# A hybrid encoder trunk on one core: gated attention as two streams, local attention divided by its sums at the gates

## The chip, the cores and the metric

The kernel runs on one core of a Trainium2 chip. The metric is the device time of one execution in microseconds; the kernel before takes 2370.76 us, the median of 3 runs (2369.61 to 2370.84). The core has five engines with a queue each: TensorE (PE in the profile, with PEld for its weight loads), VectorE (DVE), ScalarE (ACT), GpSimd (POOL) and SyncE (SP). SP issues all DMAs of this kernel, in the order of the program.

## The reference, cut to what matters

Two layers act on two sequences, 2048 and 512 tokens of width 1024. The even layer has one input projection, two parallel attention branches and one output projection; the odd layer is a gated short convolution.

```python
# branch A: gated linear attention, 4 heads of 128, in both directions
b = jnp.cumsum(gi, axis=2)                      # log decay within a chunk
inter = einsum('bhcd,bhde->bhce', qi * exp(b), S)
intra = einsum('bhij,bhje->bhie', scores, vi)   # scores: q_i . (k_j * exp(b_i - b_j))
S_new = exp(b_last) * S + einsum(..., ki * exp(b_last - b), vi)
# branch B: local attention over |i-j| <= 128, 8 heads of 64, 2 key heads
e = jnp.exp(s - m)
p = e / (jnp.sum(e, -1, keepdims=True) + jnp.exp(sk - m))
o = jnp.einsum('bnkgqs,bnskd->bnqkgd', p, vb)
return o * jax.nn.silu(z)                       # the gate
# then
x = layer_norm(DN_ALPHA * x + concatenate([ya, yb]) @ w_out)
```

The dividing by the sum in branch B can be done before the product with the values, as here, or behind it, since each query has one sum for each head.

## The kernel before, in words

All 2560 tokens are laid end to end: groups 0 to 3 (512 tokens each) are the long sequence and group 4 is the short one; a chunk `c` is 128 tokens, 20 in all.

**Dense stages.** `run` lists them in order: for groups 4, 3, 2, 1 a token stage (`tok`, values and decay inputs, weights 336 wide) and a channel stage (`ch`, 21 weight units), then the output projection of group 4 (`oe`), `tok` and `ch` of group 0, the odd layer of group 4 (`one`), `oe` 0, `oo` 4, `oe` 1, `oe` 2, then pairs of groups through the odd layer (`pair`) with the remaining `oe` and `oo`. Each dense product is made of three matmuls in fp32r, high by high, high by low and low by high. A weight unit is loaded by SP (`ws`), its high half cast by ScalarE (`wh`, three buffers) and its low half subtracted by GpSimd (`wl`, two buffers); `dense_ch` and `dense_tok` use them. What a dense stage puts out goes through PSUM banks (`acc`, four, and `ps`, four) and through the eight middle buffers `md` to DRAM.

**The order of the work** is written by a planner in Python while the program is built. `Model` keeps a clock for each engine from rough costs. The dense generator is the main stream; at each of its `yield`s `Flow.pump` lets side generators go on, those whose tiles are ready by the model and whose rank comes first (rank 0: preparing inputs; 1: gated attention; 2: local attention and the rest). `flow.defer` puts a step off until its tiles are written by the model. So PE's order is fixed in the program, and the hardware follows it with semaphores.

**Gated attention** (`gla_stream`, `inside`, lines 1186 to 1382, 1454 to 1491). Chunks go backwards, 19 to 16 and then 15 to 0. `inside` does a whole chunk: seven levels (block sizes 1 to 64), in which VectorE multiplies the decays into the queries `QQ` and the keys `KK` and PE forms scores block by block in small matmuls, 32 columns wide; then the keys are turned (`turn`), multiplied with the values (`grow`) and the state of the backward direction is brought on. `QQ`, `KK` have one buffer each, so a chunk's levels begin when the chunk before is through. Then `along` goes forward through the chunks and writes the mixed, gated output.

**Local attention** (`swa_front`, `swa_back`, lines 1510 to 1664). For each of 20 chunks and 2 key heads, `swa_front` makes the scores of four heads in `Pt`, their maximum, the exponentials and sums `den`, takes the reciprocal, and VectorE multiplies the probabilities by it, head by head. `swa_back` turns the probabilities on PE, splits them, multiplies them with the values, and GpSimd multiplies the two heads' outputs `o` by the gate `gb`. At most two blocks wait between them (`self.blocks`).

**Buffers** touched: `e2p` (one each of `QQ`, `KK`, `tA`, `v` and others, two `km`, four `P`), the four wide buffers `y` of `yp` (also: residual rows, some weights of the token stages, the decay projection's weights `up` and inputs `G`), and the eight `md`.

Of the kernel before, what the change touches and what calls it, by code (L numbers as in the profile page):

```python
# [22 lines left out]
NC = T // 128  # L23
# [239 lines left out]
class Flow:  # L263
# [113 lines left out]
class Trunk:  # L377
    def __init__(self, tc, nc, I, y_out, ctx):
# [23 lines left out]
        self.vb_s = dr("vb_s", (NC, 128, 256))  # L402
        self.qf_s = dr("qf_s", (NC, 128, 512))
# [10 lines left out]
        self.blocks = []  # L414
# [154 lines left out]
    def dense_ch(self, xh, xl, w=None, last=True):  # L569

        nc = self.nc
        wh, wl = w or self.weight()
        p = self.pd()
        for k in range(8):
            c = slice(k * 128, k * 128 + 128)
            nc.tensor.matmul(p[:], wh[:, c], xh(k), start=(k == 0), stop=False)
            nc.tensor.matmul(p[:], wh[:, c], xl(k), start=False, stop=False)
            yield
        if last:
            self.drop(wh)  # L580
            self.cook()
        for k in range(8):
            c = slice(k * 128, k * 128 + 128)
            nc.tensor.matmul(p[:], wl[:, c], xh(k), start=False, stop=(k == 7))
            if k % 2 and k < 7:
                yield
        if last:
            self.drop(wl)
        return p
# [86 lines left out]
    def setup(self):  # L676
        nc, c = self.nc, self.const
        nc.scalar.preload_act_table_set("natural_log_exp_and_others")
        load = self.load
        self.ident = load("ident", (128, 128))  # L680
        self.hl = load("hl", (128, 2))
        self.norm_g = load("norm_g", (128, 1))
        self.eps = c.tile([128, 2], F32, name="eps")
        nc.vector.memset(self.eps[:, 0:1], LN_EPS)
        nc.vector.memset(self.eps[:, 1:2], NORM_EPS)
        self.dtot = c.tile([128, NC, 4], F32, name="dtot")
        self.one = c.tile([128, 1], F32, name="one")
        nc.vector.memset(self.one[:], 1.0)
# [490 lines left out]

    def gla_load_k(self, c):  # L1180
        K = self.e((128, 2, 512), "KK")
# [4 lines left out]
    def inside(self, c, first, last, ld, K, ahead):  # L1186
# [3 lines left out]
        Q = self.e((128, 2, 512), "QQ")  # L1190
# [10 lines left out]

        acmp = self.sm((128, 4, 32), "acmp")
# [17 lines left out]
        def grow_k(s):  # L1220
# [12 lines left out]
        Sb = self.bst if not last else None  # L1233
        wait = []
        for li, s in enumerate((1, 2, 4, 8, 16, 32, 64)):
            n = 512 // s
            pls = []
            if s in (8,):
                qm = self.m2(hold=True)
                nc.scalar.copy(qm[:].rearrange("p (b two s) -> p b two s", two=2, s=s), halves(Q, s))  # L1240
                wait.append((li, s, qm))
            else:
# [14 lines left out]
                for lt, t, qm in wait:  # L1257
# [3 lines left out]
                    self.drop(qm)  # L1261
# [24 lines left out]
                kms.pop(s, None)  # L1286
# [36 lines left out]
        nc.vector.tensor_copy(self.dtot[:, c], mk(end, 4, [[1, 4]]))  # L1323
        ahead(0)
        self.flow.defer(lambda: nc.sync.dma_start(self.qf_s[c], Q[:, 1]), Q)

        def turn(i):
# [3 lines left out]
            t = self.e((128, 4, 128), "km", bufs=2)  # L1331
# [3 lines left out]
        def grow(t):  # L1335
            pv = self.pw((128, 4, 128))
            for h in range(4):
                nc.tensor.matmul(pv[:, h], t[:, h], v[:, h * 128:h * 128 + 128], start=True, stop=True)
            return pv

        kf = kb = None
        if not last:
            yield from self.bank()
# [5 lines left out]
                                  acmp[:].unsqueeze(2).broadcast_to(wide))  # L1349
        if not first:  # L1350
            yield from self.bank()
            kb = turn(1)
        ahead(1)
# [10 lines left out]
        if not first:  # L1364
# [6 lines left out]
            else:  # L1371
                for h in range(4):
                    nc.vector.scalar_tensor_tensor(Sn[:, h], Sb[:, h], mk(end, h, [[1, 1]]), pv[:, h],
# [8 lines left out]
        yield [Q]  # L1382
# [19 lines left out]
    def along(self, c, first, last, ld, ahead):  # L1402
# [13 lines left out]
        if not last:  # L1416
# [4 lines left out]
            else:  # L1421
                for h in range(4):
                    nc.vector.scalar_tensor_tensor(Sn[:, h], Sf[:, h], self.dtot[:, c, h:h + 1], m[:, h],
# [29 lines left out]

    def gla_stream(self):
        for g in (4, 3, 2, 1, 0):
# [3 lines left out]
            cs = list(range(4 * g + 3, 4 * g - 1, -1))  # L1459
            ld, K = self.gla_load(cs[0]), self.gla_load_k(cs[0])  # L1460
            nxt = {}
            for i, c in enumerate(cs):
                yield [*ld, K]

                def ahead(n):
                    if i < 3:
                        nxt[n] = (self.gla_load, self.gla_load_k)[n](cs[i + 1])
                yield from self.inside(c, *ends(c), ld, K, ahead)
                ld, K = nxt.get(0), nxt.get(1)
            if 4 * g > c0:  # L1470
                continue
            self.bst = None
            ld = K = None
            nxt.clear()
# [35 lines left out]
    def swa_front(self):  # L1510
# [16 lines left out]
        while left:  # L1527
# [10 lines left out]
            for kv in range(2):  # L1538
# [3 lines left out]
                Pt = self.e((128, 4, 385), "P", bufs=4)  # L1542
# [36 lines left out]
    def swa_back(self):  # L1579
# [17 lines left out]
        for n in range(40):  # L1597
# [4 lines left out]
            if kv == 0:  # L1602
# [3 lines left out]
                gb, o = load(c)  # L1606
            yield [Pt]
# [26 lines left out]
            yield [pl, V]  # L1634
            Pt = None
# [15 lines left out]
            yield [gb]  # L1651
# [451 lines left out]
    def run(self):  # L2103
# [70 lines left out]
        flow.add(self.swa_front())  # L2174
        flow.add(self.swa_back())
# [29 lines left out]
```

## Time and profile before

| what | value |
|---|---|
| median of 3 runs | 2370.76 us |
| the profiled execution, its own time | 2370.12 us |
| its span, first to last instruction | 2368.1 us |
| mean granted clock of TensorE | 0.998 |
| instructions | 43087 |

The page of the profile lists busy times by engine and by groups of instructions; other views answer by stretch of time, by tile, by wait. Nearly all instructions carry line 242 (the helper that notes every operation for the planner), so groups are told apart by the tiles' names: `wl<-ws,wh` is the subtraction for a weight's low half, `acc<-st,wh` a dense matmul, `ps<-QQ,km` a matmul of a level, `P<-P,den` the scaling of probabilities.

### The profile page before, as it was taken

The page shows a single profiled execution, that of the slowest core. Times are in us where ns is not written, and L with a number is a line of the kernel's source. Part 1 is how long each engine was busy: PE and PEld are TensorE (multiplying, and loading weights), DVE is VectorE, ACT ScalarE, POOL GpSimd, SP SyncE. Part 2 cuts the span into 40 slices and gives each one's busy share as a digit, 9 for nine tenths or more (in the row PEclk, how much of TensorE's full clock was granted, in tenths as well). Part 3 has the DMA queues.
Part 4 walks back from the last instruction along what each step waited for, and adds up shares of the span by engine and source line. Part 5 has one row for each costly group of instructions (what it writes and reads, how often), then busy time and mean ns, then how long its engine had stood idle before and what let it go on. Part 6 is the DMA issues. An engine that isn't in the chain of part 4 may idle for free.

```text
span 2368.1 us, 43087 instructions
## 1 busy us (share of the span) xinstructions
PE 2343.9 (99%) x15830; PEld 1951.8 (82%) x15830; DVE 1582.8 (67%) x2699; ACT 1226.1 (52%) x2363; POOL 1418.4 (60%) x1610
## 2 busy tenths in 40 slices
PE   8999999999999999999999999999999999999998
PEld 8888889888988888888888888878888877888887
DVE  2267756767767677577776467876566587656567
ACT  4666776656576645665577532543334343333431
POOL 5454435443444444444444467898887689988674
PEclk9999999999999999999999999999999999999999
DMA  7977686676667657675478777232124633221573
GB/s 230 295 226 233 221 269 229 209 221 221 218 194 236 223 173 242 197 218 161 158 245 268 266 261 243 92 116 89 52 78 140 217 105 103 73 72 58 175 242 121
DMA packets 275057, 437.37 MB, mean 185 GB/s; under 512 B 21360, under 2 KB 160240, under 8 KB 274848
## 3 DMA queue, kind: packets, MB, share of 16 engines
q1 hardware_dynamic: 274848, 434.64, 56.5%
q8 instruction: 125, 2.05, 0.4%
q14 instruction: 84, 0.69, 0.1%
HBM read 319.72 MB, written 114.84 MB: 184 GB/s over the span
## 4 chain that ended last, share of the span: by engine, by line
PE 87%; DVE 5%; POOL 4%; DMA 2%; issue 1%; ACT 1%; SPq 0%; POOLq 0%; DVEq 0%; ACTq 0%
PE acc L242 71%; PE ps L242 17%; POOL wl L242 1%; POOL wh L242 1%; DVE st L242 1%; DVE bst L242 1%; DVE y L242 1%; POOL md L242 0%; SPq L242 0%; DVE QQ L242 0%; DVE P L242 0%; DVE KK L242 0%; DMA K<-kb_s 0%; DMA mix_s<-gb 0%; DMA op_s<-QQ 0%
## 5 line engine op out<-in xcount | busy, mean ns | idle before, releaser
L242 POOL TENSOR_TENSOR wl<-ws,wh 128x256 fp32r<-128x256 f32 (+1 forms) x912 | 750.7, 855 | 711.4 <-PE acc L242 478.0
L242 PE MATMUL acc<-st,wh 128*128 128x512 f32 x3160 | 828.5, 395 | 2.8 <-DVE pr L242 2.0
L242 PEld LDWEIGHTS acc<-st,wh 128*128 128x128 f32 x3160 | 580.9, 188 | 121.0 <-issue 3.1
L242 PE MATMUL acc<-st,wl 128*128 128x512 f32 x1744 | 471.9, 395 | 2.8 <-POOL wl L242 1.9
L242 PE MATMUL acc<-wh,st 128*128 128x512 f32 (+1 forms) x1680 | 389.4, 371 | 7.9 <-ACT st L242 6.4
L242 PEld LDWEIGHTS acc<-st,wl 128*128 128x128 f32 x1744 | 320.8, 188 | 68.0 <-POOL wl L242 4.1
L242 PEld LDWEIGHTS acc<-wh,st 128*128 128x128 f32 x1680 | 300.2, 189 | 55.1 <-ACT st L242 6.4
L242 ACT CAST wh<-ws 128x1024 fp32r<-128x1024 f32 (+2 forms) x252 | 249.0, 989 | 184.2 <-DMA ws<-in_w_oo 55.9
L242 PE MATMUL acc<-wl,st 128*128 128x512 f32 (+1 forms) x840 | 209.0, 368 | 0.6 <-POOL wl L242 0.5
L242 ACT ACTIVATE md<-md 128x512 f32<-128x512 f32 x264 | 164.7, 631 | 20.5 <-DVE md L242 14.9
L242 PEld LDWEIGHTS acc<-wl,st 128*128 128x128 f32 x840 | 150.7, 188 | 23.8 <-POOL wl L242 1.3
L242 DVE SCALAR_TENSOR_TENSOR md<-acc,md 128x512 f32<-128x512 f32 (+1 forms) x113 | 77.0, 683 | 81.5 <-ACT md L242 76.5
L242 DVE TENSOR_TENSOR st<-pr,st 128x512 fp32r<-128x512 f32 x115 | 98.5, 874 | 41.6 <-ACT st L242 41.2
L242 ACT ACTIVATE md<-acc 128x512 f32<-128x512 f32 (+1 forms) x133 | 76.2, 597 | 67.0 <-PE acc L242 66.5
L242 POOL TENSOR_TENSOR wh<-md,wh 128x256 fp32r<-128x256 f32 x118 | 96.7, 842 | 13.6 <-ACT wh L242 13.1
L242 ACT CAST pth<-ps 128x512 fp32r<-128x512 f32 x112 | 65.3, 583 | 73.1 <-PE ps L242 72.3
L242 DVE CUSTOM_DVE_ANT_0 P<-ps,P 128x384 f32<-128x384 f32 (+1 forms) x160 | 79.3, 525 | 29.6 <-PE ps L242 29.0
L242 ACT ACTIVATE P<-P,nm 128x385 f32<-128x385 f32 (+1 forms) x160 | 93.2, 587 | 3.9 <-DVE nm L242 3.9
L242 ACT ACTIVATE mv<-mv,eps 128x1 f32<-128x1 f32 x40 | 11.8, 295 | 151.8 <-DVE mv L242 147.7
L242 PE MATMUL acc<-P,wh 128*128 128x512 f32 x312 | 89.5, 400 | 0.4 <-POOL wh L242 0.4
L242 ACT COPY km<-KK 128x512 f32<-128x512 f32 x80 | 50.8, 635 | 72.2 <-DVE KK L242 50.9
L242 ACT CAST st<-pr 128x512 fp32r<-128x512 f32 x115 | 68.3, 617 | 30.3 <-DMA pr<-mix_s 12.9
(490 smaller groups left out, 4090.2 us busy)
## 6 DMA issues: line engine op xcount, KB each, us to landing
ws<-in_w_ch SPq DMA_DIRECT2D x105, 512.0 KB, 4.4
ws<-in_w_od SPq DMA_DIRECT2D x58, 512.0 KB, 4.2
ws<-in_w_oe SPq DMA_DIRECT2D x40, 512.0 KB, 3.8
ws<-in_w_oo SPq DMA_DIRECT2D x36, 512.0 KB, 3.5
K<-kb_s SPq DMA_DIRECT2D x32, 384.0 KB, 6.3
d_s<-md SPq DMA_DIRECT2D x40, 256.0 KB, 4.2
qb_s<-md SPq DMA_DIRECT2D x80, 128.0 KB, 3.9
tA<-d_s SPq DMA_DIRECT2D x20, 512.0 KB, 5.7
```

Source lines behind the costliest of these rows:

```text
L242: r = f(*a, **k)
```

## The change

1. **Two streams for gated attention.** `inside` ends after the levels and the copy of the totals; it puts the chunk on `self.heads`. A new stream `gla_behind` takes it from there through `behind` (turned keys, values, states). At most two chunks may be open (`self.open`).
2. **Buffers for that.** Keys and queries are taken and dropped explicitly; `gla_home` gives their own buffer or, where that is taken, one of the wide `y` buffers, though not between the end of group 1's projections and the loading of the residual rows of group 4. Compacted keys `km` may also lie in `md`; the turned keys always do.
3. **Loads.** The next chunk's decays are loaded at level 4 and its keys at level 32, across group borders where the inputs are there; values are loaded by the second stream.
4. **Local attention divides at the gates.** The four multiplies on `Pt` go. The reciprocals go to DRAM (`rd_s`) by one DMA for each block, and `swa_back` loads them broadcast over 64 partitions by four DMAs for each block into a buffer of `md`; GpSimd multiplies the gate by it before the multiply with `o`.
5. **Ranks.** Both streams of gated attention and both of local attention have rank 1.
6. **The planner.** `flush` looks each late step up again before it runs it, and `dense_ch` holds its bank until it is done.

```diff
     def flush(self, everything=False, name=None):
-        now, keep = [], []
-        for one in self.late:
-            (now if everything or name in one[2] or (name is None and one[0] <= self.t) else keep).append(one)
-        self.late = self.model.late = keep
+        now = [one for one in self.late if everything or name in one[2] or (name is None and one[0] <= self.t)]
         for one in now:
-            one[1]()
+            if any(one is x for x in self.late):
+                self.late[:] = [x for x in self.late if x is not one]
+                one[1]()
...
+    def gla_home(self, tag):
+
+        done = self.flow.done
+        rows = "swa_in1" in done and "res_x1_4_3" not in done
+        return [(self.e2, tag, 1)] if rows or self.model.spare(tag, 1) else self.large[:1]
+
     def gla_load_k(self, c):
-        K = self.e((128, 2, 512), "KK")
+        K = self.take(self.gla_home("KK"), (128, 2, 512))
...
-        Q = self.e((128, 2, 512), "QQ")
+        while self.free_at(self.gla_home("QQ")) > self.flow.t:
+            yield 0.3
+        Q = self.take(self.gla_home("QQ"), (128, 2, 512))
...
+        while self.open > 1:
+            yield 0.3
+        self.open += 1
...
-                    km = kms[2 * s] = self.e((128, 512), "km", bufs=2)
+                    km = kms[2 * s] = self.take([(self.e2, "km", 2)] + self.mids, (128, 512))
...
-            if s == 4:
-                v = self.e((128, 512), "v")
-                nc.sync.dma_start(v[:], self.v_s[c])
+            if s in (4, 32):
+                ahead(s)
             yield [Q] if s < 16 else [Q, K]
-        end = tots[128]
+        nc.vector.tensor_copy(self.dtot[:, c], mk(tots[128], 0, [[1, 8]]))
+        self.heads.append((c, first, last, K, Q, base, acmp))
+        self.flow.mark("head_%d" % c)
...
+    def behind(self, c, first, last, K, Q, base, acmp, v, ahead):
...
-            t = self.e((128, 4, 128), "km", bufs=2)
+            t = self.m2((128, 4, 128), hold=True)
             nc.scalar.copy(t[:], pt[:])
...
+    def gla_behind(self):
+        nxt = []
+        for c in [*range(19, 15, -1), *range(15, -1, -1)]:
+            yield "head_%d" % c
+            v = nxt.pop() if nxt else self.load_v(c)
...
+            yield from self.behind(*self.heads.pop(0), v, ahead)
...
-                Pt = self.e((128, 4, 385), "P", bufs=4)
+                Pt = self.new(self.e2, (128, 4, 385), F32, "P", 4, True)
...
                 nc.vector.reciprocal(den[:], den[:])
-                for h in range(4):
-                    nc.vector.tensor_scalar(Pt[:, h, :w], Pt[:, h, :w], den[:, h:h + 1], None, op0=ALU.mult)
-                    if h == 1:
-                        yield []
+                nc.sync.dma_start(self.rd_s[c, kv].rearrange("h t -> t h"), den[:])
...
+            if kv == 0:
+                rb = self.m2(hold=True)
+            for j in range(4):
+                nc.sync.dma_start(rb[64 * kv:64 * kv + 64, 128 * j:128 * j + 128],
+                                  self.rd_s[c, kv, j:j + 1].broadcast_to([64, 128]))
...
-            yield [gb]
+            yield [gb, rb]
+            flat = gb[:].rearrange("p h t -> p (h t)")
+            nc.gpsimd.tensor_tensor(flat, flat, rb[:], op=ALU.mult)
+            self.drop(rb)
+            yield [o]
             nc.gpsimd.tensor_tensor(gb[:], o[:], gb[:], op=ALU.mult)
...
         flow.add(self.gla_stream(), rank=1)
-        flow.add(self.swa_front())
-        flow.add(self.swa_back())
+        flow.add(self.gla_behind(), rank=1)
+        flow.add(self.swa_front(), rank=1)
+        flow.add(self.swa_back(), rank=1)
```

More of the change, by code (lines that the diff above doesn't have):

```diff
@@ L413, in __init__ @@
         self.bst = None
-        self.blocks = []
+        self.blocks, self.heads, self.open = [], [], 0
         self.x, self.owned, self.refs, self.pairs, self.wblocks = {}, {}, {}, {}, {}
@@ L572, in dense_ch @@
         wh, wl = w or self.weight()
-        p = self.pd()
+        p = self.pd(hold=True)
         for k in range(8):
@@ L1232, in inside @@
         base = None
-        Sb = self.bst if not last else None
         wait = []
@@ L1338, in grow, with place @@
                 nc.tensor.matmul(pv[:, h], t[:, h], v[:, h * 128:h * 128 + 128], start=True, stop=True)
+            self.drop(t)
             return pv
+        def place():
+            yield from self.bank()
+            while self.free_at(self.mids) > self.flow.t:
+                yield 0.3
         kf = kb = None
         if not last:
-            yield from self.bank()
+            yield from place()
             kf = turn(0)
@@ L1349, in inside @@
                                   acmp[:].unsqueeze(2).broadcast_to(wide))
+        self.open -= 1
         if not first:
-            yield from self.bank()
+            yield from place()
             kb = turn(1)
-        ahead(1)
+        self.drop(K)
         yield [A, v] + ([Sb] if Sb is not None else [])
@@ L1452, in seq, with ahead @@
         return (0, 16) if g < 4 else (16, 20)
+    def gla_behind(self):
[3 more added lines that the diff above has]
+            v = nxt.pop() if nxt else self.load_v(c)
+            def ahead():
+                if c not in (0, 16) and "gla_in%d" % ((c - 1) // 4) in self.flow.done:
+                    nxt.append(self.load_v(c - 1))
+            yield from self.behind(*self.heads.pop(0), v, ahead)
+            v = None
     def gla_stream(self):
+        nxt = {}
         for g in (4, 3, 2, 1, 0):
```

56 lines of the change are left out of this document (38 added, 18 removed).

## The prediction

> **What bounds the kernel now.** I read the page first: the span, the busy row, the chain that ended last, and the counts of DMA packets.
>
> ```profile
> span 2368.1 us, 43087 instructions
> ...
> PE 2343.9 (99%) x15830; PEld 1951.8 (82%) x15830; DVE 1582.8 (67%) x2699; ACT 1226.1 (52%) x2363; POOL 1418.4 (60%) x1610
> ...
> DMA packets 275057, 437.37 MB, mean 185 GB/s; under 512 B 21360, under 2 KB 160240, under 8 KB 274848
> ...
> q1 hardware_dynamic: 274848, 434.64, 56.5%
> ...
> PE 87%; DVE 5%; POOL 4%; DMA 2%; issue 1%; ACT 1%; SPq 0%; POOLq 0%; DVEq 0%; ACTq 0%
> ```
>
> PE is busy for 2343.9 of 2368.1 us, so all its idle time is 24.2 us, and 87% of the chain is PE. An average over stages hides where the 24.2 us lie, so next comes the view by stretches (columns: window, us, busy us and instruction count of PE, PEld, DVE, ACT, POOL, then clock, DMA share, GB/s). Below it stand the first and the last group of attention's matmuls, by their tiles (ns least/median/most, first and last start): they run from 121.9 to 1357.3 us.
>
> ```profile
> 0.00:100.00 100.00, 93.40 (x460) 81.24 (x461) 25.78 (x47) 55.74 (x89) 54.53 (x84) 1.00 0.81 251
> 100.00:1300.00 1200.00, 1198.14 (x10694) 1008.12 (x10693) 842.75 (x1767) 755.15 (x1577) 536.47 (x672) 1.00 0.69 220
> ...
> 1500.00:1600.00 100.00, 97.00 (x412) 77.67 (x411) 81.40 (x95) 41.97 (x73) 92.28 (x86) 0.98 0.26 90
> ...
> 1900.00:2000.00 100.00, 96.45 (x423) 77.35 (x423) 87.74 (x103) 40.60 (x75) 91.21 (x85) 1.00 0.28 96
> ...
> 2300.00:2368.00 68.00, 60.20 (x263) 48.91 (x261) 43.70 (x61) 12.56 (x27) 31.78 (x37) 0.97 0.40 145
> ...
> L242 PE MATMUL ps<-qn,KK x640: 196/196/218, 121.9 to 1140.9; 128*32 128x32 f32 x160
> L242 PE MATMUL ps<-ident,km x80: 270/272/273, 320.9 to 1357.3; 128*128 128x128 f32 x80
> ```
>
> This is the main reading. In the 1200 us in which attention runs, PE idles 1200 − 1198.14 = 1.86 us. The rest of its idle time is the first load (6.6), the tail (7.8), and two places of 3.0 and 3.55 us in the pair stages. VectorE, with 843 of 1200 us, has room. What PE waited for says the same (us in total, times, longest):
>
> ```profile
> PE acc L242 <- ACT st L242: 6.4, 1, 6.4
> PE acc L242 <- POOL wl L242: 2.4, 3, 1.1
> ```
>
> No row names an attention tile at over 1 us. Attention is filler between the dense matmuls, and filler that finishes sooner shortens nothing unless something dense waits for it. Its first consumer in the last stretch is the output projection of group 0, whose input is loaded from the mixed values (SP row) and used by PE (second row) at:
>
> ```profile
> 1263.46 1.60 SPq L242 DMA_DIRECT2D pr<-mix_s  x3
> ...
> 1319.65 2.54 PE L242 MATMUL acc<-wh,st 128*128 128x512 f32 x10
> ```
>
> The load is issued 56 us before PE turns to that stage, and PE is still in the stage before until then. Attention being earlier is worth nothing there; being later costs something only after some 50 us.
>
> **The change part by part.** *PE.* No matmul, transpose or weight load is removed or added: levels, turned keys, values, states and the eight-head scores keep their counts, so the 15830 stay. That term is 0.
>
> *Order on PE.* Two chunks may now be open and local attention is sorted by ready time beside them. The price of mixing is in the time line: eight dense matmuls take 1.98 us after others like them, and 2.11 us after a burst of small ones.
>
> ```profile
> 539.79 1.98 PE L242 MATMUL acc<-st,wh 128*128 128x512 f32 x8
> ...
> 541.70 0.46 PE L242 MATMUL ps<-qn,KK 128*32 128x32 f32 x32
> 541.97 0.56 PE L242 MATMUL ps<-QQ,KK 128*32 128x32 f32 x32
> 542.46 2.11 PE L242 MATMUL acc<-st,wh 128*128 128x512 f32 x8
> ...
> L242 PE MATMUL ps<-QQ,KK 128*32 128x32 f32 (+1 forms) x1600 | 34.1, 210 | 0.1
> L242 PE MATMUL ps<-QQ,km 128*32 128x32 f32 x1920 | 28.1, 199 | 1.1 <-ACT pth L242 0.7 <-DVE acmp L242 0.2 <-DVE QQ L242 0.2
> L242 PE MATMUL ps<-qn,KK 128*32 128x32 f32 x640 | 9.2, 199 | 0.0
> L242 PE MATMUL ps<-md,km 128*32 128x32 f32 x640 | 9.2, 199 | 0.0
> ```
>
> That is 0.13 us for each return. The four groups have 4800 small matmuls; in bursts of 32 these are at most 150 returns, 20 us. But the levels of one chunk still follow each other in one stream, and the other stream has only wide matmuls, so bursts can hardly meet more often. I take 0, with a quarter of the 20 us as the bound each way (an estimate): −5 to +5.
>
> *VectorE.* The scaling of the probabilities goes, and on the page of the attention stretch with shapes kept apart it is two rows. The sums' reciprocals stay.
>
> ```profile
> L242 DVE TENSOR_SCALAR P<-P,den 128x384 f32<-128x384 f32 x128 | 61.6, 543 | 1.1
> L242 DVE TENSOR_SCALAR P<-P,den 128x256 f32<-128x256 f32 x32 | 10.9, 405 | 0.3
> ...
> L242 POOL TENSOR_TENSOR wl<-ws,wh 128x256 fp32r<-128x256 f32 x564 | 459.8, 847 | 541.3 <-PE acc L242 385.4 <-ACT wh L242 103.9 <-ACT km L242 9.8
> L242 POOL TENSOR_TENSOR gb<-gb 128x512 f32<-128x512 f32 x20 | 27.3, 1367 | 61.4 <-DVE gb L242 61.4
> ```
>
> So 61.6 + 10.9 = 72.5 us leave an engine that PE does not wait for: worth 0 up to the 1.86 us of idle time. I take −0.5. The copy of the totals takes eight columns for four: nothing.
>
> *GpSimd.* A multiply of 128x512 is added for each of 20 chunks: 20 × 1.367 = 27.3 us. Queued behind it are the subtractions that make the weights' low halves, and PE waits for those. But GpSimd stands idle for 385.4 us in front of them until PE gives a buffer back, so 1.4 us at a time lies beside that: 0. Were this cover gone it would be the whole 27.3. The new multiply waits for gates and factors only, and stands ahead of the old one, which waits 61.4 us in 15 places for VectorE; some of it fills that.
>
> *SP's queue.* This is the one new wait with something behind it. For each of 40 blocks one store of the reciprocals is issued at once, not deferred, so SP stands until the reciprocal is done; and four broadcast loads follow (160 in all), which must wait until the store has landed. 200 issues at the 0.33 to 0.62 us of the rows below (a fifth of 3.11) are 66 to 124 us more on SP. Behind them stand the loads of weights: for those ScalarE's cast waits, then GpSimd, then PE. How late may a weight load be? One unit, followed through four engines:
>
> ```profile
> 543.17 0.33 SPq L242 DMA_DIRECT2D ws<-in_w_ch  x1
> ...
> 549.31 1.04 ACT L242 CAST wh<-ws 128x1024 fp32r<-128x1024 f32 x1
> ...
> 554.02 3.89 POOL L242 TENSOR_TENSOR wl<-ws,wh 128x256 fp32r<-128x256 f32 x4 [4.21 <-PE acc L242]
> ...
> 564.86 0.62 PE L242 MATMUL acc<-st,wl 128*128 128x512 f32 x2
> ...
> ws<-in_w_ch SPq DMA_DIRECT2D x105, 512.0 KB, 4.4
> ...
> 709.21 3.11 SPq L242 DMA_DIRECT2D kb_s<-md  x5
> ...
> SPq L242 <- DVE den L242: 9.1, 3, 4.5
> SPq L242 <- POOL wl L242: 490.1, 195, 7.4
> ...
> DMA to landing us min/median/max: 2.7/4.7/6.7
> ```
>
> It lands at 543.2 + 4.4 = 547.6; the cast could wait 1.7 us more for it; between cast and subtraction lie 554.02 − 550.35 = 3.7 us; between subtraction and use 564.86 − 557.91 = 6.9 us. Together 12.3 us of cover. The new wait is bounded by 4.5 us (the longest that SP now waits for a den tile) plus a landing of 4.7, the median of the mixed values' transfers: about 9 us, and nothing where the block lies queued first. Waits of SP up to 7.4 us are there already, 195 of them, and PE does not feel them. So the wide stages hide it. The four token stages after the first have narrower weights and less cover: of 40 blocks over some 1070 us, about 6 fall into their 4 × 40 us. From 0 to 6 × 4 us; I take a quarter of a microsecond each, +1.5.
>
> The Trainium skill speaks against this store: its page "DMA: Bandwidth & Descriptors", section "Specifications", says that transfers under 512 B are read, changed and written back. The store has 512 pieces of 4 B, and the 20480 new ones would nearly double the page's 21360 packets under 512 B. At the price of an average packet here, 0.565 × 16 × 2368.1 us / 274848 = 78 ns, one store takes 512 × 78 / 16 = 2.5 us, and the landing 7.2. The wait is then 11.7 us, just inside the cover, and the sum by this rule would be about 2 us higher. No row here prices such a piece.
>
> *Buffers.* Keys and queries take a second home among the four wide buffers (y), the compacted keys, the turned keys and the factors come from the eight middle ones (md). These also take what the dense stages put out. An eviction that finds none free holds ScalarE and then a bank; today no bank is waited for longer than the rows above. I take 0; the upper bound is the second rival.
>
> *The planner's own edits* (late work run once, the dense bank held, one rank) issue nothing. Their effect is in the order, bounded above.
>
> **Sum.** The profiled execution took 2370.1 us, 2.0 outside its span; the median of the runs is 0.6 above it. 2370.1 + 0 − 0.5 + 0 + 1.5 + 0 = 2371.1. I write **2371 us**: no change that can be told.
>
> **Rivals.** *The pair stages gain* (faster): with attention done sooner, buffers come free and both stalls go, 3.0 + 3.55 us, and with the granted clock of 0.98 in the first of them another 2: 2371 − 8.5 = 2362. Against it: the second stall, at 1900 to 2000, has the same size with no attention for 500 us, and both follow GpSimd's load (92 and 91%).
>
> *SP's queue starves PE* (slower). Place: the store that waits for the reciprocal and the loads that wait for the store. It decides when the two waits of successive blocks fall on one weight, over 12 us. If in half of the 40 blocks PE is left 0.8 us without weights, that is 16 us: 2387. For it: SP is strictly in order, and the planner knows nothing of a wait in DRAM. Against: the cover above.
>
> *The wide buffers* (slower). The residual rows of the first output projection need all four of them:
>
> ```profile
> L242 SPq DMA_DIRECT2D y<-in_x x4: 423/425/498, 763.9 to 800.5; - x4
> ...
> L242 DVE SCALAR_TENSOR_TENSOR y<-y,acc x6: 669/683/690, 825.2 to 869.4; 128x512 f32<-128x512 f32 x6
> ```
>
> The last row is loaded 25 us before its first use. It decides if keys or queries hold such a buffer past 825: the dense stream then stands, some 10 to 20 us, 2381 to 2391. The change bars keys and queries from them before that stage, which speaks against it. A stall of this length would also cost clock: in the stretch 1500 to 1600, with 3.0 us idle, the granted clock fell to 0.98.
>
> *It doesn't speed attention up*: the streams wait for the dense stage that makes their input, or for each other. The time is the same 2371, since nothing dense waits for it.
>
> **How the numbers follow.** A measurement of this kernel tells about 0.2%, 4.7 us, from no change, so "same" is 2366.0 to 2375.5. No change, whether attention is sooner or not: 0.46. The pair stages, or an order that is luckier by about as much: 0.24. SP's queue 0.18, the buffers 0.12. So faster 0.24, same 0.46, slower 0.30. The range goes from 2359 (the faster case with the lower bound of the order) to 2388 (SP's case), which leaves out the far half of each.
>
> **What would show it.** Right: 15830 matmuls; PE idle in the attention stretch under 5 us; VectorE 70 us less busy; GpSimd 27 us more; the last attention matmul before 1357 and the pair stage starting where it does. Wrong: rows in which PE waits for the casts, the subtractions or the wide buffers for over 5 us in sum; SP waiting for a landing of the reciprocals for over 12 us; or fewer or cheaper dense matmuls in the attention stretch, which I exclude.

## The result, and the profile after

The changed kernel takes 2528.82 us (median of six runs, 2521.07 to 2536.77) against 2370.03 us for the kernel before (six runs, 2369.05 to 2370.84). The ratio is 1.0668, with a 95% interval of 1.0644 to 1.0692: 159 us slower. The prediction was 2371 us in a range of 2359 to 2388, so it was wrong, by far more than the range.

The profiled execution took 2522.22 us. Its page, in the same lines as before (the last is the traffic of SP's queue: packets, MB, share of 16 DMA engines):

```profile
span 2520.4 us, 43271 instructions
...
PE 2389.7 (95%) x15830; PEld 1980.6 (79%) x15830; DVE 1507.1 (60%) x2539; ACT 1224.8 (49%) x2364; POOL 1442.3 (57%) x1630
...
DMA packets 309124, 442.74 MB, mean 176 GB/s; under 512 B 45056, under 2 KB 194432, under 8 KB 308912
...
q1 hardware_dynamic: 308912, 439.98, 61.5%
```

PE does the same 15830 matmuls. Its idle time went from 24.2 to 2520.4 − 2389.7 = 130.7 us, 106.5 more. Its busy time went up by 45.8 us with no more work: the mean granted clock fell from 0.998 to 0.980, and 2343.9 × 0.998 / 0.980 is 2387. The two add up to the 152 us by which the span grew. VectorE has 75.7 us less to do. The DMA engines move only 5.4 MB more, but 23696 more packets are under 512 B.

The view by stretches says where (columns as in the prediction):

```profile
0.00:100.00 100.00, 93.41 (x460) 81.32 (x461) 25.78 (x47) 55.74 (x89) 53.92 (x84) 1.00 0.81 250
100.00:1300.00 1200.00, 1113.23 (x10056) 926.94 (x10054) 695.19 (x1457) 666.14 (x1332) 497.32 (x614) 0.97 0.77 198
1300.00:1500.00 200.00, 177.58 (x865) 148.41 (x866) 98.33 (x190) 115.22 (x333) 84.62 (x106) 0.94 0.76 223
1500.00:1600.00 100.00, 99.37 (x438) 81.69 (x437) 63.99 (x78) 32.49 (x54) 66.76 (x72) 1.00 0.73 249
```

Until attention begins nothing differs. From 100 to 1300 PE idles 86.8 us, where it idled 1.9, and from 1300 to 1500, with attention still running, another 22.4. After that it is as full as before.

What PE waited for there (us in total, times, longest) names no one culprit:

```profile
PE ps L242 <- DMA tA<-qf_s: 14.0, 3, 6.1
PE ps L242 <- DMA QQ<-qf_s: 11.1, 3, 9.5
PE ps L242 <- DVE QQ L242: 8.9, 4, 4.6
PE ps L242 <- DMA pr<-x_s: 8.7, 2, 8.2
...
PE acc L242 <- ACT wh L242: 4.9, 2, 3.7
```

All sorts of loads come late, so one looks upstream, at SP's waits (first three rows) and, in the same view for all engines, at ScalarE's wait for weights (last row; it was 43.0 us in 19 waits before):

```profile
SPq L242 <- POOL wl L242: 384.9, 143, 8.1
...
SPq L242 <- DMA rd_s<-den: 119.8, 24, 9.7
...
SPq L242 <- DVE den L242: 82.7, 25, 6.6
```

```profile
ACT wh L242 <- DMA ws<-in_w_ch: 109.4, 37, 7.8
```

The two new waits of SP are the ones that the prediction named. They are also the obvious story: SP waits, loads come late. It is the wrong one, as the time line of SP and the stretches around one store show (start, duration; then the stretch columns):

```profile
540.92 0.37 SPq L242 DMA_DIRECT2D rd_s<-den  x1
541.38 3.25 SPq L242 DMA_DIRECT2D ws<-in_w_ch  x2
544.73 0.39 SPq L242 DMA_DIRECT2D d_s<-md  x1
...
549.63 0.33 SPq L242 DMA_DIRECT2D v<-v_s  x1
```

```profile
533.00:541.00 8.00, 8.00 (x100) 6.50 (x99) 4.65 (x9) 6.98 (x12) 3.56 (x5) 1.00 0.95 316
541.00:549.00 8.00, 8.00 (x110) 6.68 (x109) 6.28 (x11) 4.01 (x8) 3.27 (x4) 1.00 0.22 25
549.00:557.00 8.00, 8.00 (x40) 6.67 (x39) 1.75 (x7) 2.94 (x5) 1.76 (x3) 1.00 0.76 240
```

Right behind the store SP issues two loads of weights, 1 MB in all, the second of them by 544.63 us. Yet in the 8 us after the store all DMA engines together move 25 GB/s, that is 0.2 MB; in the 8 us before they moved 316. SP's order does not explain that: the requests are there, and next to nothing flows.

That holds for the other stores too: averaged from 4 to 10 us behind its issue, none of the 40 leaves more than 141 GB/s. The table gives the rate of all transfers of the core in steps of 2 us around a store's issue, as the mean over the 40 stores, worked out from the trace's packets (GB/s; e4, e5, e7 and e10 are experiments below):

| us from the issue | −4 | −2 | 0 | 2 | 4 | 6 | 8 | 10 | 12 |
|---|---|---|---|---|---|---|---|---|---|
| after | 258 | 204 | 149 | 114 | 54 | 33 | 44 | 131 | 305 |
| e4, 4 B pieces side by side | 221 | 166 | 186 | 140 | 59 | 37 | 53 | 169 | 307 |
| e7, 4 B pieces 512 B apart | 211 | 154 | 152 | 207 | 235 | 250 | 230 | 222 | 190 |
| e10, 4 B pieces 64 B apart | 218 | 154 | 152 | 202 | 235 | 257 | 222 | 234 | 181 |
| e5, 16 B pieces side by side | 211 | 158 | 165 | 155 | 236 | 272 | 233 | 236 | 189 |

### The profile page after: what moved, and what is told of

Read it like the earlier page. It is cut to its first block, busy times and chain, and to the rows that moved or that the text cites. A ratio compares the mean times of both kernels' runs of the same rounds, so it can differ in the third digit from the quotient of the medians.

```text
span 2520.4 us, 43271 instructions
## 1 busy us (share of the span) xinstructions
PE 2389.7 (95%) x15830; PEld 1980.6 (79%) x15830; DVE 1507.1 (60%) x2539; ACT 1224.8 (49%) x2364; POOL 1442.3 (57%) x1630
## 5 line engine op out<-in xcount | busy, mean ns | idle before, releaser
L242 DVE TENSOR_TENSOR ptl<-ps,pth 128x512 fp32r<-128x512 f32 x112 | 76.2, 681 | 43.1 <-ACT pth L242 43.1
L242 PE MATMUL ps<-K,Q 128*128 128x384 f32 (+1 forms) x320 | 73.4, 343 | 13.5 <-DVE mx L242 7.0
```

What stands on the lines that cost most here:

```text
L242: r = f(*a, **k)
```

## The experiments

The theory after this first look: the store of the reciprocals, 512 pieces of 4 B (2 KB in all), costs the time by holding up everybody's transfers, not by SP's waiting. The rivals: SP's two waits, for the reciprocal and for the landing of the store; the four broadcast loads; the two streams and their borrowed buffers; the order that the planner makes of it. The question behind: what in the store is dear.

| run | time, us | ratio to before, 95% |
|---|---|---|
| e1_scale_back | 2365.45 | 0.9985 (0.9976 to 0.9994) |
| e1_again | 2366.11 | 0.9986 (0.9977 to 0.9995) |
| e2_gates_only | 2583.40 | 1.0901 (1.0883 to 1.0920) |
| e4_store_only | 2532.89 | 1.0685 (1.0667 to 1.0703) |
| e5_store_rows | 2390.28 | 1.0089 (1.0074 to 1.0104) |
| e7_store_apart | 2391.16 | 1.0095 (1.0081 to 1.0109) |
| e10_apart64 | 2391.78 | 1.0095 (1.0081 to 1.0109) |
| e8_load_pieces | 2369.96 | 1.0002 (0.9992 to 1.0011) |
| e3_rows16 | 2375.15 | 1.0025 (1.0016 to 1.0035) |
| e6_turned_rows | 2385.89 | 1.0072 (1.0059 to 1.0085) |
| e9_late | 2374.86 | 1.0024 (1.0014 to 1.0034) |
| e12_held | 2380.17 | 1.0049 (1.0036 to 1.0063) |

None of them leaves out a part of the computation. e4, e5, e7, e8 and e10 add a transfer whose data nobody uses, and VectorE's scaling stays in them.

**Which half of the change (e1, e1 again, e2).** e1 keeps the streams, buffers, ranks and planner edits of the changed kernel and puts the scaling back:

```diff
-                nc.sync.dma_start(self.rd_s[c, kv].rearrange("h t -> t h"), den[:])
+                for h in range(4):
+                    nc.vector.tensor_scalar(Pt[:, h, :w], Pt[:, h, :w], den[:, h:h + 1], None, op0=ALU.mult)
+                    if h == 1:
+                        yield []
...
-            if kv == 0:
-                rb = self.m2(hold=True)
-            for j in range(4):
-                nc.sync.dma_start(rb[64 * kv:64 * kv + 64, 128 * j:128 * j + 128],
-                                  self.rd_s[c, kv, j:j + 1].broadcast_to([64, 128]))
...
-            yield [gb, rb]
-            flat = gb[:].rearrange("p h t -> p (h t)")
-            nc.gpsimd.tensor_tensor(flat, flat, rb[:], op=ALU.mult)
-            self.drop(rb)
-            yield [o]
+            yield [gb]
```

> The changed kernel with VectorE's scaling of the probabilities put back and the store, the loads and the second gate multiply taken out; the two streams, their buffers and the one rank stay. If the store of 4-byte pieces (theory A) or the waits of SP's queue for it (theory B) made the 158 us, this takes 2365 to 2385 us with PE idle under 10 us between 100 and 1300. If the streams and their buffers made it (theory C), it stays above 2480.

e2 is the other half: the kernel before with the same edit the other way round (store, four loads, second multiply, no scaling), and none of the rest.

> The kernel before with only the division moved to the gates (store, four loads, second multiply), one stream, old ranks. Theories A and B: 2480 to 2540, and after each store the DMA's rate falls to some 25 GB/s for 8 us. Theory C: 2365 to 2385.

e1 was run once more later, beside other runs of the kernel before:

> The changed kernel with the scaling put back once more, on the same chip as the late one: 2363 to 2368, that is 0.998 to 0.999 of the kernel before.

e1 took 2365.45 us and 2366.11 us: 3.7 and 2.4 us less than the kernel before beside it, and both intervals end below 1. e2 took 2583.4, above the 2480 to 2540 that were expected. So the whole loss, and more, is the division at the gates; the rest of the change (streams, buffers, ranks and the planner's edits) wins a little. The stretches of e1, and then of e2:

```profile
100.00:1300.00 1200.00, 1199.16 (x10709) 1010.34 (x10708) 837.81 (x1769) 756.05 (x1589) 536.93 (x673) 1.00 0.69 220
1300.00:1500.00 200.00, 200.00 (x941) 167.11 (x940) 127.86 (x167) 84.62 (x173) 132.50 (x146) 1.00 0.75 249
```

```profile
100.00:1300.00 1200.00, 1064.76 (x9341) 888.29 (x9340) 647.88 (x1347) 630.04 (x1249) 466.66 (x591) 0.94 0.75 189
```

In e1 PE idles 0.84 us in 1200, and gated attention ends sooner: its last store of mixed values starts at 1347.5 us in e1 and at 1358.4 in the kernel before. That of local attention starts later, at 1270.6 for 1261.1. How much of the 2 to 4 us comes from gated attention's earlier end is not shown; PE had only 1.86 us to win in that stretch. e2 loses 214 us where the full change loses 159, with the same 40 stores; why the streams and ranks soften it by 55 us was not followed up.

**The store alone (e4).** The kernel before, with the store added and read by nobody, so that no load depends on it:

```diff
                 nc.vector.reciprocal(den[:], den[:])
+                nc.sync.dma_start(self.rd_s[c, kv].rearrange("h t -> t h"), den[:])
                 for h in range(4):
```

> The kernel before with one more thing: the reciprocals are stored in 512 pieces of 4 bytes for each of 40 blocks and nobody reads them; VectorE still scales. Theory A (the pieces hold up the transfers of everybody): 2450 to 2530, with the same silence after each store. Theory B (SP stands until the store has landed): nothing waits for the landing here, so only SP's wait for the reciprocal is left, under 2385.

It took 2532.89 us, just above the range of theory A. A store of 2 KB for each of 40 blocks, whose data nobody reads, costs 163.7 us: as much as the whole change. SP is not quite free of it, against what was expected: the trace puts 15 of its waits down to the landing of the store.

```profile
SPq L242 <- DMA rd_s<-den: 28.8, 15, 5.0
```

Those are 28.8 us in all where the changed kernel has 119.8, and none is longer than the 7.4 us that SP waited at times in the kernel before. With that the loads' wait for the landing, the broadcast loads and the multiply on GpSimd are all out as main causes. In the attention stretch of e4 PE idles 91.8 us:

```profile
100.00:1300.00 1200.00, 1108.24 (x9761) 926.31 (x9760) 731.68 (x1553) 655.96 (x1299) 481.79 (x609) 0.96 0.74 190
```

**What in the store is dear (e5, e7, e10, e8).** The same added store with three other layouts in DRAM. e5 writes 128 pieces of 16 B, so that each partition's four sums lie together; e7 writes the 512 pieces of 4 B each 512 B from the next, e10 each 64 B from the next. Only the shape of `rd_s` and the view of it differ; first e5 against e4, then e7 (in e10 the last 128 is 16):

```diff
-        self.rd_s = dr("rd_s", (NC, 2, 4, 128))
+        self.rd_s = dr("rd_s", (NC, 2, 128, 4))
...
-                nc.sync.dma_start(self.rd_s[c, kv].rearrange("h t -> t h"), den[:])
+                nc.sync.dma_start(self.rd_s[c, kv], den[:])
```

```diff
-        self.rd_s = dr("rd_s", (NC, 2, 4, 128))
+        self.rd_s = dr("rd_s", (NC, 2, 4, 128, 128))
...
-                nc.sync.dma_start(self.rd_s[c, kv].rearrange("h t -> t h"), den[:])
+                nc.sync.dma_start(self.rd_s[c, kv, :, :, 0].rearrange("h t -> t h"), den[:])
```

> As the store nobody reads, but the same 2048 bytes go as 128 pieces of 16 bytes. Theory A with a price for each piece: a quarter of the silence, about 2 us for each store, 2370 to 2395. If the price were in the bytes or in the wait for the reciprocal, the same time as with 512 pieces.

> The kernel before with the store that nobody reads, 512 pieces of 4 bytes, each 512 bytes from the next in DRAM. If each small piece has its price wherever it goes, 2510 to 2550 as with neighbouring pieces (2533). If the price is that neighbouring pieces, sent by different engines, meet in the same stretch of DRAM, under 2400.

> The kernel before with the store that nobody reads, its 512 pieces of 4 bytes 64 bytes apart in DRAM (512 apart gave 2391, neighbours 2533, with the same order of instructions on all engines). If pieces disturb each other only within 64 bytes, 2385 to 2397. If the stretch is 512 bytes, 2420 to 2533.

e5, e7 and e10 took 2390.28, 2391.16 and 2391.78 us. In e4, e5, e7 and e10 every engine has the same instructions in the same order, and e4, e7 and e10 the same 512 pieces of 4 B. So 2532.89 − 2391.16 = 141.7 us, 3.5 us for each store, come from one thing alone: that the pieces are neighbours in DRAM. SP's wait for the reciprocals is not it either: it is 115.4 us in all in e4 and 130.3 in e7. A distance of 64 B is enough to be rid of it, and so are pieces of 16 B that do touch.

The first store of e4 and of e7, issued at 163.37 and at 163.81 us, shows how PE comes to lose by it. Stretches of e4 and then of e7:

```profile
165.00:173.00 8.00, 8.00 (x51) 7.58 (x49) 0.20 (x2) 3.51 (x6) 4.14 (x8) 1.00 0.46 47
173.00:181.00 8.00, 4.61 (x78) 4.41 (x78) 5.30 (x9) 2.56 (x5) 1.26 (x2) 0.69 0.62 207
```

```profile
165.00:173.00 8.00, 8.00 (x51) 7.67 (x50) 3.48 (x9) 4.58 (x8) 3.75 (x8) 1.00 0.78 240
173.00:181.00 8.00, 8.00 (x140) 7.49 (x139) 6.42 (x11) 2.93 (x6) 4.85 (x7) 1.00 0.19 39
```

In both, SP issues the same six transfers behind the store. In e7 data move at 240 GB/s at once; in e4 at 47, and at 207 in the next 8 us, in which PE idles 3.4 us and its granted clock falls to 0.69. The low rate of e7 in its second stretch harms nobody: PE is busy for 8.00 of 8 us.

e8 asks whether it is small pieces as such, with a load in place of the store, 512 pieces of 4 B from an input into a tile that nobody uses:

```diff
                 nc.vector.reciprocal(den[:], den[:])
+                dm = self.sm((128, 4), "dm")
+                nc.sync.dma_start(dm[:], self.I["mline"][0:4, 0:128].rearrange("h t -> t h"))
```

> The kernel before with a load that nobody reads in the place of that store: 512 pieces of 4 bytes from DRAM into 128 partitions, for each of 40 blocks. If only writes of small pieces are dear, 2366 to 2385; if any small piece is, 2480 or more.

It took 2369.96 us: no difference that can be told. (In e8 PE, VectorE, ScalarE and GpSimd have the instructions of the kernel before, in the same order.) Neighbouring pieces are dear where they are written, not where they are read.

What stays is 21 to 23 us of e5, e7 and e10 over the kernel before. Their stretches (e5, then e7, then e10) show it in another place:

```profile
100.00:1300.00 1200.00, 1198.77 (x10667) 1007.70 (x10666) 826.83 (x1730) 737.43 (x1505) 547.69 (x676) 1.00 0.68 214
1300.00:1500.00 200.00, 191.24 (x872) 156.63 (x871) 124.59 (x183) 85.61 (x228) 108.52 (x127) 0.97 0.81 266
```

```profile
100.00:1300.00 1200.00, 1198.25 (x10664) 1007.48 (x10663) 828.81 (x1729) 736.17 (x1505) 547.88 (x675) 1.00 0.68 214
1300.00:1500.00 200.00, 191.61 (x862) 156.81 (x861) 123.22 (x182) 85.84 (x229) 106.05 (x125) 0.96 0.79 262
```

```profile
100.00:1300.00 1200.00, 1199.42 (x10672) 1008.36 (x10671) 826.88 (x1731) 737.81 (x1506) 547.13 (x678) 1.00 0.68 214
```

While the stores run, PE idles 0.6 to 1.8 us, no more than before, although SP stands some 130 us for the reciprocals in each. PE then idles 8 to 9 us between 1300 and 1500, when the stores are over, and in all three 5.7 us of that is the same wait for tiles of gated attention:

```profile
PE ps L242 <- ACT km L242: 5.7, 2, 3.1
```

Gated attention ends late there. These are its stores of mixed values (first and last start) in the kernel before and then in e7:

```profile
L242 SPq DMA_DIRECT2D mix_s<-qn x10: 524/525/847, 334.1 to 1358.4; - x10
L242 SPq DMA_DIRECT2D mix_s<-qn x10: 524/525/525, 343.9 to 1419.7; - x10
```

That is 61 us later, and the prediction put the slack at some 50. The added store moves the planner's clock of SP, and the order of the program around it changes. That this different order is what delays gated attention is argued, not shown: SP's wait for the reciprocals could do it too, and e8 has neither.

**Can the division at the gates be had cheaply (e3, e6, e9)?** e3 is the changed kernel with pieces of 16 B and one broadcast load for each block:

```diff
-        self.rd_s = dr("rd_s", (NC, 2, 4, 128))
+        self.rd_s = dr("rd_s", (NC, 2, 128, 4))
...
-                nc.sync.dma_start(self.rd_s[c, kv].rearrange("h t -> t h"), den[:])
+                nc.sync.dma_start(self.rd_s[c, kv], den[:])
...
-            for j in range(4):
-                nc.sync.dma_start(rb[64 * kv:64 * kv + 64, 128 * j:128 * j + 128],
-                                  self.rd_s[c, kv, j:j + 1].broadcast_to([64, 128]))
+            nc.sync.dma_start(rb[64 * kv:64 * kv + 64, :],
+                              self.rd_s[c, kv].rearrange("t h -> (t h)").unsqueeze(0).broadcast_to([64, 512]))
...
-            nc.gpsimd.tensor_tensor(flat, flat, rb[:], op=ALU.mult)
+            nc.gpsimd.tensor_tensor(gb[:], gb[:], rb[:].rearrange("p (t h) -> p h t", h=4), op=ALU.mult)
```

> The changed kernel with the reciprocals stored as 128 pieces of 16 bytes and loaded by one broadcast for each block instead of four. By the store that nobody reads (2390 with such pieces) and the two streams' -4: 2380 to 2395.

e6 turns the reciprocals on PE first and stores four rows of 512 B:

```diff
-                nc.sync.dma_start(self.rd_s[c, kv].rearrange("h t -> t h"), den[:])
+                yield [den]
+                yield from self.bank()
+                pr = self.pw()
+                nc.tensor.transpose(pr[:4, :128], den[:], self.ident[:])
+                rs = self.m2()
+                nc.scalar.copy(rs[:4, :128], pr[:4, :128])
+                yield [rs]
+                nc.sync.dma_start(self.rd_s[c, kv], rs[:4, :128])
```

> The changed kernel with one difference: PE turns the reciprocals, and the store writes four rows of 512 bytes. Everything else of the change stays, the loads and the second gate multiply too. If the pieces of the store are the whole loss, this takes 2362 to 2372 us, as the kernel with the scaling put back (2365), and the 72 us that VectorE is spared are worth nothing. If the loads or the waits for them cost by themselves, 2380 to 2420.

e3 took 2375.15 us, less than expected: 153.7 of the 158.8 us are gone with the layout of the store (and the fewer loads). e6 took 2385.89, in its second range; its DMA rate shows no silence (188 to 238 GB/s in the steps after a store), so what it has over e3 comes with the turning, the copying, the four loads or the order that they bring, which were not separated. SP's waits in e3 fit this:

```profile
SPq L242 <- DVE den L242: 106.1, 29, 6.5
...
SPq L242 <- DMA rd_s<-den: 6.6, 5, 2.7
```

The wait for the landing was 119.8 us in the changed kernel and is 6.6 here: it was a symptom, since e4 has 28.8 and loses as much. The wait for the reciprocal is longer here (106.1 for 82.7), and the kernel is 154 us faster all the same.

But e3 is 9 us above e1, although its VectorE has less to do. e9 puts e3's two waits of SP out of the way: it yields for `den` ahead of the store, and issues the broadcast load when the block's values are done.

```diff
                 nc.vector.reciprocal(den[:], den[:])
+                yield [den]
                 nc.sync.dma_start(self.rd_s[c, kv], den[:])
...
-            nc.sync.dma_start(rb[64 * kv:64 * kv + 64, :],
-                              self.rd_s[c, kv].rearrange("t h -> (t h)").unsqueeze(0).broadcast_to([64, 512]))
...
                 old = (kb, ph, pl)
                 yield []
+            nc.sync.dma_start(rb[64 * kv:64 * kv + 64, :],
+                              self.rd_s[c, kv].rearrange("t h -> (t h)").unsqueeze(0).broadcast_to([64, 512]))
             yield [pl, V]
```

> The changed kernel with the reciprocals stored as 128 pieces of 16 bytes only once the planner holds them to be done, and loaded by one broadcast for each block after the block's last values instead of before its first. If the 10 us that the version with such pieces (2375) stands above the one with the scaling put back (2365) are waits of SP's queue, they go: 2362 to 2368. If the second gate multiply or the buffer held for the factors makes them, 2372 to 2378. Under 2362 would mean that the 72 us taken from VectorE are worth something after all.

It took 2374.86 us, no better. Its waits for the reciprocal fell to 42.5 us and those for the landing to 0.9:

```profile
SPq L242 <- DVE den L242: 42.5, 25, 4.8
...
SPq L242 <- DMA rd_s<-den: 0.9, 1, 0.9
```

So SP's waits, 113 us in e3 and 43 in e9, make no difference. e12 goes the other way round: e1 with neither store nor loads, but with the buffer held from one block to the next, filled with ones by VectorE (20 fills of 485 ns), and the second multiply on GpSimd.

```diff
+            if kv == 0:
+                rb = self.m2(hold=True)
+                nc.vector.memset(rb[:], 1.0)
...
-            yield [gb]
+            yield [gb, rb]
+            flat = gb[:].rearrange("p h t -> p (h t)")
+            nc.gpsimd.tensor_tensor(flat, flat, rb[:], op=ALU.mult)
+            self.drop(rb)
+            yield [o]
```

> The kernel with the scaling put back, with the middle buffer for the factors held as in the change and the second gate multiply done, but the buffer is filled with ones by VectorE: no store of reciprocals and no load. If the 9 us by which the versions with cheap stores (2375) stand above the one with the scaling put back (2365) come from the held buffer or from GpSimd's second multiply, 2372 to 2378; if they come from the transfers and from SP's queue, 2363 to 2368.

It took 2380.17 us, 14 above e1 and above both expected ranges, with no transfer added. So a loss of this size needs no DMA: in e12 it lies with the held `md` buffer, the fills, the second multiply, or the order that they bring about. Which of these was not separated. Its stretches show 3.5 us of idle time in the first and 5.05 in the second, where e1 has 0.84 and 0:

```profile
100.00:1300.00 1200.00, 1196.50 (x10683) 1006.52 (x10683) 849.60 (x1778) 749.71 (x1573) 561.91 (x691) 1.00 0.68 217
1300.00:1500.00 200.00, 194.95 (x880) 160.10 (x879) 124.14 (x164) 80.20 (x175) 121.61 (x134) 0.97 0.77 256
```

But e3 and e9 do not lose their time there. Their first stretches (e3, then e9) show 6.4 and 8.0 us of idle time, and their second ones 0.7 and 0.6:

```profile
100.00:1300.00 1200.00, 1193.63 (x10671) 1006.04 (x10670) 775.22 (x1601) 750.91 (x1585) 570.17 (x687) 1.00 0.70 223
```

```profile
100.00:1300.00 1200.00, 1191.99 (x10681) 1003.71 (x10680) 781.66 (x1617) 758.60 (x1613) 562.73 (x685) 1.00 0.72 226
```

So e12 does not show that the 9 us of e3 and e9 come from the same thing; what costs them stays open.

**The fastest version** is e1, the two streams with VectorE's scaling: 0.9985 and 0.9986 of the kernel before in two sets of runs.

## Why the prediction was wrong

**The step that failed** is the term for SP's queue, +1.5 us, in "one store of the reciprocals ... and four broadcast loads follow (160 in all), which must wait until the store has landed". It asked how long SP would stand and how long the store itself would take to land, and set that against 12.3 us of cover. What it never asked is what the store does to the transfers of others. e4 shows that this alone makes a loss as large as the whole: nobody reads its store, and it loses 163.7 us. In place of 1.5 the term measured 142 us (e4 against e7, the layout alone) to 154 us (the change against e3).

The wait itself misled. I bounded its two parts at 4.5 us for the reciprocal and 4.7 for the landing, about 9 together; the longest were 6.6 and 9.7, so both bounds were too low. Still the prediction's sign of error, "SP waiting for a landing of the reciprocals for over 12 us", would not have gone off. Others did: PE idles 86.8 us in the attention stretch where under 5 would have been right, and its waits for casts, subtractions and wide buffers are 4.9, 1.2 and 5.5 us, over 5 in sum. The cover of 12.3 us was counted for one weight that comes late by itself. But for some 8 us after a store, as around 541 us above, hardly a weight, decay, query or gate arrives, and PE waits for all kinds of loads.

**The rule of the Trainium skill** (page "DMA: Bandwidth & Descriptors", section "Specifications": transfers under 512 B are read, changed and written back) pointed at the right instruction. The price that I put on it was wrong: 78 ns a piece, an average packet's, gave a store of 2.5 us, and it was charged to that store alone. The runs also say that a size under 512 B is not by itself the condition of this loss: e7 and e10 write the same 4 B pieces and e5 writes 16 B pieces, and none of them has the silence. The measurement decides here: 4 B pieces that touch are dear, and 64 B apart they are not; distances between these were not run. The same page of the Trainium skill, section "Rules for kernel authors", says that a strided last dimension becomes one descriptor for each element, and to rearrange it. The 23696 new packets under 512 B agree with that, and e3, which rearranges, takes 2375 us. I had read past this rule.

**Term by term.** *PE, 0*: right; 15830 matmuls. *Order, −5 to +5*: e1, which has the streams, is at −2.4 and −3.7, inside. *VectorE, −72.5 us of work, worth −0.5*: the work was right, 75.7 us less. Its worth is not separated: e3 and e9, which have that relief, are 9 us above e1, which has not, but they carry the second multiply and the held buffer too. *GpSimd, 27.3 us, hidden*: the size was right (20 multiplies of 1349 ns in the row below are 27.0), but that it costs nothing is not borne out: e12 pays 14 us for the multiply, the held buffer and its fills together. *Buffers, 0*: those of the streams are in e1 and cost nothing; that of the factors is open for the same reason.

```profile
L242 POOL TENSOR_TENSOR gb<-gb,md 128x512 f32<-128x512 f32 x20 | 27.0, 1349 | 2.9 <-DVE KK L242 2.7 <-issue 0.2
```

**The rivals.** "SP's queue starves PE", at 0.18 and 2387 us, had the place (the store, then the weights) and the direction; its mechanism, two waits of SP that fall on one weight, is not what costs: e4 has 28.8 us of waits for the landing for 119.8 and loses as much, and e7 has e4's wait for the reciprocal without the loss. "The wide buffers" at 2381 to 2391 is not it: e1 has them and is faster than before. "The pair stages gain" did not come: in e1 gated attention ends 11 us sooner, and both stalls of 3.0 and 3.55 us are still there, at 3.0 and 3.31 us (the stretches below). "It doesn't speed attention up ... nothing dense waits for it" fits e1 in its second half: gated attention does end 11 us sooner, and e1 as a whole gains only 2 to 4.

```profile
1500.00:1600.00 100.00, 97.00 (x413) 77.71 (x412) 81.81 (x98) 40.04 (x70) 92.28 (x87) 0.98 0.27 93
...
1900.00:2000.00 100.00, 96.69 (x423) 77.79 (x422) 86.15 (x102) 43.10 (x77) 92.71 (x86) 1.00 0.28 95
```

**The range.** It was built of waits alone, each bounded by a row of the trace. The one operation with no row like it, a write of 4 B pieces, got a price of its own, so its upper bound was 24 us. The prediction itself said "No row here prices such a piece"; that should have opened the range upward, and not closed it at an average packet. (Its lower end, 2359, is not the sum that it names either: 2362 − 5 is 2357. Nothing hangs on that here.)

## What to carry to other kernels

A small DMA is not priced by its bytes, nor by how long its issuer waits: ask how many pieces it has, whether it writes them side by side, and what else is in flight, since it may hold up everybody. Here a turned store of 2 KB cost 3.5 us of kernel time each time. With each partition's values together, and the turning left to the engine that reads them, the whole kernel (e3) stands 6 us above the kernel before for all 40 blocks. When many kinds of loads come late at once, look at the DMA rate around each issue before believing a row of waits, and take the suspect's readers away to see whether the loss goes with them.

## What the runs showed of the hardware

- **Writes of 4 B side by side hold up all of the core's transfers.** After each such store of 512 pieces the core's 16 DMA engines together moved 33 to 59 GB/s from 4 to 10 us behind its issue, where the same pieces 64 or 512 B apart left 222 to 257. The cost was 141.7 us for 40 stores (e4 against e7), 141.1 against 64 B apart. Reading 512 pieces of 4 B cost nothing that can be told (e8: 2369.96 us beside 2369.30), and pieces of 16 B side by side no more than 4 B pieces that lie apart (e5 against e7 and e10).
- What the cause is below this level stays open. Whether it takes two DMA engines that write in one stretch of 64 B, or only many pieces in one, was not tried. e5 has four pieces in 64 B and is cheap, e4 sixteen.
- The trace's own time for a 4 B packet is 9 ns (median), so the store's own packets do not show it. The others do: the 4 KB packets that start 6 to 8 us behind a store take 603 ns in the median in the changed kernel and 588 in e4, where 159 is the median of either run.
- **A short stall costs clock too.** In e4 PE idles 3.4 us from 173 to 177; the clock granted then is 0.77, 0.50, 0.50 and 0.52 in the four steps of 2 us from 175 on, with PE busy again from 177:

```profile
173.00:175.00 2.00, 0.48 (x33) 0.35 (x32) 0.00 (x0) 0.00 (x0) 0.00 (x0) 1.00 0.84 302
175.00:177.00 2.00, 0.12 (x8) 0.13 (x12) 1.41 (x2) 0.00 (x0) 0.00 (x0) 0.77 0.98 327
177.00:179.00 2.00, 2.00 (x37) 1.94 (x38) 2.00 (x6) 0.62 (x1) 0.00 (x0) 0.50 0.49 154
179.00:181.00 2.00, 2.00 (x9) 2.00 (x9) 1.90 (x4) 1.94 (x4) 1.26 (x2) 0.50 0.16 43
181.00:183.00 2.00, 2.00 (x9) 2.00 (x9) 1.97 (x5) 0.65 (x2) 2.00 (x3) 0.52 0.00 1
```

That is how 106.5 us of idle time became 152 in the changed kernel: of the other 45.8 some 43 are, by the mean clock, PE at work with a lower clock.
